# A hybrid encoder layer on one core: wide products of a unit ahead of its small ones, recurrence work moved from GpSimd to VectorE, and a new tail

## The chip, the cores and the metric

One core of a Trainium2 chip runs the whole layer. The metric is the device time of one execution in microseconds (us); lower is better. The engines are TensorE (PE, with its weight loads PEld), VectorE (DVE), ScalarE (ACT), GpSimd (POOL) and SyncE (SP), which issues most of the DMAs. Line numbers are those of the profiled kernel unless a text says that they are the changed kernel's.

## The reference

One layer for S = 256 tokens of width D = 2048, all in fp32:

```
x = x + 1/2 * SwiGLU_1(RMSNorm(x))                 # w1, w3: 2048 -> 5632, w2: 5632 -> 2048
h = RMSNorm(x);  [q | k | v | u | y] = h @ W_in     # 8 query heads, 2 kv heads of 128; u, y: 1024
A = attention(q, k, v), per-head RMS norm of q and k, axial rotary
u = centred depthwise conv of width 4 (u)
R = (RG-LRU_fwd(u) + RG-LRU_bwd(u)) * gelu(y)
x = x + concat([A, R]) @ W_out
x = x + 1/2 * SwiGLU_2(RMSNorm(x))
x = x + sigmoid(RMSNorm(x) @ W_gate) * (p @ W_ple)
out = RMSNorm(x)
```

The RG-LRU of one direction: r and i are sigmoids of u times block-diagonal matrices of 128 x 128 plus a bias; a = exp(c * r), where c comes from lambda; b = sqrt(1 - a^2) * i * u; and h[t] = a[t] * h[t-1] + b[t] along the tokens.

## The kernel before, in words

**Products.** The activations lie transposed, features on the partitions and the 256 tokens along a row. Every fp32 weight tile is split into a high part `whi` in fp32r (a cast on ACT, L83) and a low part `wlo` (a subtraction on VectorE, L84), and the activations likewise, as [hi | lo], 512 columns. A product is then a *wide* matmul, `whi` times 512 columns (L115), and a *small* one, `wlo` times the 256 hi columns (L117); `total` adds the two halves of the accumulator. `unit` makes 128 output features out of 16 weight tiles, or of two runs of 11 for w2. One 1 MB DMA on SP brings a unit's weights into one of three raw buffers, and two split pairs of eight tiles each go into a pool of four. Within a unit the order is 8 wide, 8 small, 8 wide, 8 small (for w2: 8, 8, 3, 3 in each run). After a unit `tick` moves every open job (a Python generator) one step on; the emitted instructions then get their final place on each engine from the Tile scheduler.

**Stages.** FFN1 runs to some 762 us: its lead takes the first units piece by piece with x, in pieces of 1, 1, 2, 4, 4, 4 blocks, the first three of them on ACT's DMA queue and the rest on SP's between the weight pieces. An FFN goes through the hidden width in two halves: 22 units of w1 and 22 of w3 give the hidden blocks `hT`, then 16 units of w2 add to x. Then the mixing stage, to 965 us, in this order: eight units of W_in for u, in two groups g of four, each followed by a convolution (L370) and the start of its `scan_job`; the projection of k and v; the two of q with rotary embedding; eight units for y; then wout, to 1055 us. FFN2 follows to some 1790 us, the gate with the embedding of p to 1890, and the tail.

**Scan job.** For a group of 512 features and both directions it makes four gate tiles: split uc and the gate weights (ACT and POOL), three fp32r products of 256 columns for each of 32 gate blocks over both jobs (L91 to L93), sigmoids (L403), products with c on POOL (L407), Exp and Tanh on ACT, i * u on POOL (L413), Sqrt on ACT, (a + 1) * r on VectorE (L419), times i * u on POOL (L421), four scans of 256 on VectorE (L424), and for both directions together the sum on POOL (L427). The final `y_job` multiplies with gelu(y) and splits into `mixT`, the activations of wout. POOL also scales u and y (L437, L574) and does one product of each rotary (L461).

**Tail.** The last two gate units keep their weights; their wide products come by halves of 128 tokens (L656), each followed by its features' sums, its norm (L209), a row of factors made on PE, and the scaling of all of x (L639) ahead of the stores. The output leaves in feature layout, which the host turns.

## Time and profile before

| | before |
|---|---|
| median of 3 runs | 1907.63 us (1907.08 to 1908.33) |
| the profiled execution | 1907.39 us, span 1905.6 us |
| PE / DVE / ACT / POOL busy | 98% / 63% / 51% / 15% of the span |
| mean granted clock of TensorE | 0.993 of full speed |
| HBM | 349 MB read, 2.1 MB written, 184 GB/s over the span |

The profile is of one execution, whose own time stands beside its span: a sum over its rows is made against that. Busy times of engines overlap. A matmul's end is modelled, so a run of matmuls is timed by the distance from its start to the start of the next run. A clock of 1.00 is TensorE at 2.4 GHz, the lower level is 1.2 GHz. In the waits, [0.71 <-DVE aT L88] means that the engine stood idle for 0.71 us, until VectorE's write of aT at line 88.

### The profile page before, as it was taken

Reading aid. Unit: us, or ns where it says so; the run is one execution under the profiler, and the core shown is the slowest. Engines: PE = TensorE matmul, PEld = TensorE weight load, DVE = VectorE, ACT = ScalarE, POOL = GpSimd, SP = SyncE. Lnnn points to the kernel's source line nnn. Section 1 sums busy time; section 2 is a strip of 40 time slices with the busy share of each in tenths; the row PEclk is TensorE's granted clock in tenths of the full one; section 3 lists DMA queues with packets and bytes.
Section 4 is the critical chain, followed back from the end, with each engine's and each line's share of the span. In section 5 each row is a group of like instructions: output and inputs, shape, how many; then the busy total and the mean of one; then the engine's idle time right before and its main releaser. Section 6 shows DMA issues by size and latency. Waiting matters only on the chain.

```text
span 1905.6 us, 27228 instructions
## 1 busy us (share of the span) xinstructions
PE 1872.7 (98%) x10632; PEld 1640.3 (86%) x10632; DVE 1203.6 (63%) x1723; ACT 965.2 (51%) x1494; POOL 292.6 (15%) x225
## 2 busy tenths in 40 slices
PE   9999999999999999988999999999999999999997
PEld 7888888888888888867878888888888888888886
DVE  6766655556566556888767666655555666655686
ACT  6544444444444445677654544444444444555553
POOL 0111100011111001564211111110001111101143
PEclk9999999999999999999999999999999999999998
DMA  8555545655555556544345555555565555555552
GB/s 316 205 189 187 192 160 190 210 199 179 197 180 176 182 184 213 175 152 155 133 152 181 191 185 194 182 186 167 194 208 196 181 195 184 202 197 195 201 177 67
DMA packets 61552, 352.85 MB, mean 185 GB/s; under 512 B 6512, under 2 KB 12144, under 8 KB 31088
## 3 DMA queue, kind: packets, MB, share of 16 engines
q1 hardware_dynamic: 60848, 350.51, 54.0%
q8 instruction: 83, 1.36, 0.3%
q10 hardware_dynamic: 576, 0.61, 0.1%
q14 instruction: 45, 0.37, 0.1%
HBM read 349.00 MB, written 2.10 MB: 184 GB/s over the span
## 4 chain that ended last, share of the span: by engine, by line
PE 92%; DVE 3%; ACT 3%; issue 1%; POOL 1%; DMA 0%; SPq 0%; POOLq 0%; DVEq 0%; ACTq 0%
PE acc L115 59%; PE acc L117 30%; DVE wlo L84 1%; DVE gate L424 1%; DVE uc L370 0%; ACT whi L83 0%; PE po L522 0%; PE acc L656 0%; PE pe L115 0%; POOL us L437 0%; DMA xs<-in_xT 0%; PE tr L495 0%; ACT gate L403 0%; ACT a L410 0%; ACT L416 0%
## 5 line engine op out<-in xcount | busy, mean ns | idle before, releaser
L84 DVE TENSOR_TENSOR wlo<-raw,whi 128x1024 fp32r<-128x1024 f32 x722 | 806.5, 1126 | 594.7 <-ACT whi L83 577.5
L83 ACT CAST whi<-raw 128x1024 fp32r<-128x1024 f32 x722 | 687.0, 952 | 814.5 <-PE acc L115 553.9
L115 PE MATMUL acc<-aT,whi 128*128 128x512 f32 x3296 | 832.0, 393 | 1.2 <-DVE aT L88 1.2
L115 PEld LDWEIGHTS acc<-aT,whi 128*128 128x128 f32 x3296 | 593.1, 189 | 107.8 <-DVE aT L88 2.7
L117 PEld LDWEIGHTS acc<-aT,wlo 128*128 128x128 f32 x3296 | 451.4, 191 | 32.7
L117 PE MATMUL acc<-aT,wlo 128*128 128x256 f32 x3296 | 463.0, 283 | 0.0
L115 PE MATMUL acc<-hT,whi 128*128 128x512 f32 x1408 | 364.8, 392 | 0.0
L304 POOL TENSOR_TENSOR s<-s,rB 128x256 f32<-128x256 f32 x88 | 123.8, 1407 | 1067.7 <-ACT s L301 1061.9
L115 PEld LDWEIGHTS acc<-hT,whi 128*128 128x128 f32 x1408 | 247.6, 189 | 37.2
L117 PEld LDWEIGHTS acc<-hT,wlo 128*128 128x128 f32 x1408 | 202.7, 190 | 21.3
L117 PE MATMUL acc<-hT,wlo 128*128 128x256 f32 x1408 | 209.0, 282 | 0.0
L246 POOL TENSOR_TENSOR ssq<-ssq,sqr 128x256 f32<-128x256 f32 x58 | 54.4, 939 | 339.6 <-ACT sqr L245 339.6
L115 PE MATMUL acc<-mixT,whi 128*128 128x512 f32 x256 | 64.6, 393 | 1.4 <-DVE mixT L84 1.4
L115 PEld LDWEIGHTS acc<-mixT,whi 128*128 128x128 f32 x256 | 45.9, 189 | 10.2 <-DVE mixT L84 2.1
L315 DVE SCALAR_TENSOR_TENSOR xs<-acc,xs 128x256 f32<-128x256 f32 x128 | 53.3, 417 | 0.0
L87 ACT ACTIVATE aT<-xs,par_sb 128x256 fp32r<-128x256 f32 x64 | 31.5, 506 | 41.9 <-DVE xs L315 39.3
L92 PE MATMUL acc<-wlo,aT 128*128 128x512 f32 x96 | 40.4, 421 | 11.3 <-DVE wlo L84 11.3
L88 DVE SCALAR_TENSOR_TENSOR aT<-xs,par_sb,aT 128x256 fp32r<-128x256 f32 x64 | 38.2, 610 | 19.4 <-ACT aT L87 19.1
L306 DVE TENSOR_TENSOR u<-u,s 128x256 f32<-128x256 f32 x88 | 37.4, 426 | 9.1 <-DVE u L149 0.5
L93 PE MATMUL acc<-whi,aT 128*128 128x512 f32 x96 | 39.8, 415 | 0.0
L84 DVE TENSOR_TENSOR hT<-u,hT 128x256 fp32r<-128x256 f32 x88 | 38.0, 431 | 1.9 <-ACT hT L83 1.9
L300 DVE TENSOR_TENSOR z<-z,rB 128x256 f32<-128x256 f32 x88 | 37.4, 425 | 2.7
(168 smaller groups left out, 1001.5 us busy)
## 6 DMA issues: line engine op xcount, KB each, us to landing
raw<-in_w2a SPq DMA_DIRECT2D x64, 704.0 KB, 4.0
raw<-in_w1b SPq DMA_DIRECT2D x44, 1024.0 KB, 4.8
raw<-in_w3b SPq DMA_DIRECT2D x44, 1024.0 KB, 4.9
raw<-in_w2b SPq DMA_DIRECT2D x64, 704.0 KB, 4.0
raw<-in_w3a SPq DMA_DIRECT2D x43, 1024.0 KB, 4.8
raw<-in_w1a SPq DMA_DIRECT2D x42, 1024.0 KB, 4.8
raw<-in_win SPq DMA_DIRECT2D x16, 1024.0 KB, 4.9
raw<-in_wout SPq DMA_DIRECT2D x16, 1024.0 KB, 4.8
```

The costliest lines, as they stand in the source:

```text
L83: nc.scalar.copy(hi, src)
L84: (eng or nc.vector).tensor_tensor(lo, src, f32(hi), op=ALU.subtract)
L88: nc.vector.scalar_tensor_tensor(lo, src, gain, f32(hi), op0=ALU.mult, op1=ALU.subtract)
L92: nc.tensor.matmul(ps, lhsT=ah, rhs=wl, start=False, stop=False)
L93: nc.tensor.matmul(ps, lhsT=al, rhs=wh, start=False, stop=last)
L115: nc.tensor.matmul(ps, lhsT=ws[i][0], rhs=acts[i], start=first and i == 0, stop=False)
L117: nc.tensor.matmul(ps[:, 1, :], lhsT=ws[i][1], rhs=acts[i][:, 0, :], start=False, stop=last and i == n - 1)
L246: (eng or nc.gpsimd).tensor_tensor(ssq[:, cols], ssq[:, cols], t, op=ALU.add)
L300: nc.vector.tensor_tensor(z, z, rB, op=ALU.mult)
L304: nc.gpsimd.tensor_tensor(s, s, rB, op=ALU.mult)
L306: nc.vector.tensor_tensor(u, u, s, op=ALU.mult)
L315: nc.vector.scalar_tensor_tensor(xs[:, n, :], ps[:, j, :], 0.5, xs[:, n, :], op0=ALU.mult, op1=ALU.add)
```

## The change

1. `unit` runs the wide products of all sixteen (or eleven) tiles of a weight load first, then all small ones; `tick` comes after each eight wide ones, so twice in a unit.
2. Lead: the parameters are loaded first, on SP; only the first two pieces of x go on ACT's queue (`EARLY` 3 to 2), the third goes on SP's; the ACT table load follows the first DMA; six warming products instead of eight.
3. `scan_job`: the gate products are plain fp32, without splits; the gate weights are loaded in halves in SP's order; every POOL operation is on VectorE; it yields at more points. The scalings by `rmB` and the rotary product go to VectorE too.
4. The order of mixing is u(0), k and v, u(1), q, y(0), y(1); `finish` runs open jobs to the point that y or wout needs. wout's rows are in another order on the host, and its first two units go by halves.
5. Tail: the features of both halves come back to back, squares and gains are on ACT, x is transposed on PE and scaled by the norm on the way out of PSUM, in eight pieces of 128x512 on ACT and VectorE; the output is in the layout of the reference.

```diff
-WARM = 8
...
+MIX_ORDER = [*range(4), *range(8, 12), *range(4, 8), *range(12, 16)]
...
+WARM = 6
...
-EARLY = 3
+EARLY = 2
...
+    def finish(done=lambda: not jobs):
+        while not done():
+            tick()
...
         at, n = 0, nk * len(srcs)
         for src in srcs:
             ws = weights(src, nk)
+            part = aT[at:at + nk]
             for j in range(0, nk, 8):
-                part = ws[j:j + 8]
-                unit_mms(ps, part, aT[at:at + len(part)], at == 0, at + len(part) == n)
-                at += len(part)
-        tick()
+                for i in range(j, min(nk, j + 8)):
+                    nc.tensor.matmul(ps, lhsT=ws[i][0], rhs=part[i], start=at + i == 0, stop=False)
+                tick()
+            for i in range(nk):
+                nc.tensor.matmul(ps[:, 1, :], lhsT=ws[i][1], rhs=part[i][:, 0, :], start=False,
+                                 stop=at + i == n - 1)
+            at += nk
         return ps
...
                         first=(g == 0 and k == 0), last=(g == n - 1 and k == 3))
-            tick()
+                if k % 2:
+                    tick()
         return ps
...
-    at = 0
-    for n in PIECES[:EARLY]:
-        load(flat(xs[:, at:at + n, :]), xT[:, at * S:(at + n) * S], nc.scalar)
-        if at == 0:
-            load(par_sb, par, nc.scalar)
-        at += n
+    load(par_sb, par)
+    load(flat(xs[:, 0:1, :]), xT[:, 0:S], nc.scalar)
     warm = sml.tile([P, 1], F32, tag="warm", name="warm", bufs=1)
     nc.gpsimd.memset(warm, 0.0)
     nc.scalar.activation(warm, warm, AF.Silu)
+    load(flat(xs[:, 1:2, :]), xT[:, S:2 * S], nc.scalar)
     zero = tok.tile([P, C], BF16, tag="tmp", name="zero", bufs=TMP)
     nc.vector.memset(zero, 0.0)
...
     def scan_job(g, u):
-        hi = mid.tile([P, 4, S], F32R, tag="mid", name="uc_hi")
-        lo = mid.tile([P, 4, S], F32R, tag="mid", name="uc_lo")
-        split(u, hi, lo, nc.gpsimd)
-        raw = wraw.tile([P, 4, C], F32, tag="raw", name="raw")
-        in_order(nc.sync.dma_start(flat(raw), lruw[g]), loads[-1])
-        yield
         gw = []
         for d in range(2):
-            wh = mid.tile([P, 2, C], F32R, tag="mid", name="gw_hi")
-            wl = mid.tile([P, 2, C], F32R, tag="mid", name="gw_lo")
-            split(raw[:, 2 * d:2 * d + 2, :], wh, wl, nc.gpsimd)
-            gw.append((wh, wl))
+            w = mid.tile([P, 2, C], F32, tag="mid", name="gw")
+            load(flat(w), lruw[g, :, 2 * C * d:2 * C * (d + 1)])
+            gw.append(w)
         yield
         r, i, a = [], [], []
         for d in range(2):
-            wh, wl = gw[d]
             for m in range(2):
...
-                        wc = slice(k * P, (k + 1) * P)
-                        mm3(ps[:, j, :], wh[:, m, wc], wl[:, m, wc], hi[:, k, :], lo[:, k, :],
-                            True, True)
+                        nc.tensor.matmul(ps[:, j, :], lhsT=gw[d][:, m, k * P:(k + 1) * P], rhs=u[:, k, :],
+                                         start=True, stop=True)
                     for j in range(2):
...
+                    yield
                 (r, i)[m].append(o)
-                yield
             cb = cneg[:, 8 * d + 4 * g:8 * d + 4 * g + 4].unsqueeze(2).broadcast_to([P, 4, S])
-            nc.gpsimd.tensor_tensor(r[d], r[d], cb, op=ALU.mult)
+            nc.vector.tensor_tensor(r[d], r[d], cb, op=ALU.mult)
+            yield
         for d in range(2):
...
-            nc.gpsimd.tensor_tensor(flat(i[d]), flat(i[d]), flat(u), op=ALU.mult)
-        yield
+            nc.vector.tensor_tensor(flat(i[d]), flat(i[d]), flat(u), op=ALU.mult)
+            yield
         for d in range(2):
...
-            nc.gpsimd.tensor_tensor(flat(r[d]), flat(r[d]), flat(i[d]), op=ALU.mult)
+            yield
+            nc.vector.tensor_tensor(flat(r[d]), flat(r[d]), flat(i[d]), op=ALU.mult)
+            yield
             for k in range(4):
...
-            yield
-        nc.gpsimd.tensor_tensor(flat(i[0]), flat(i[0]), flat(i[1]), op=ALU.add)
+                if k % 2:
+                    yield
+        nc.vector.tensor_tensor(flat(i[0]), flat(i[0]), flat(i[1]), op=ALU.add)
         hsum[g] = i[0]
     hsum = [None, None]
-    for g in range(2):
+    def u_part(g):
         u = mtile("uc")
...
-            nc.gpsimd.tensor_tensor(t, t, rmB, op=ALU.mult)
+            nc.vector.tensor_tensor(t, t, rmB, op=ALU.mult)
             conv(u[:, k, :], t, 4 * g + k)
         jobs.append(scan_job(g, u))
...
-        nc.gpsimd.tensor_tensor(sv, sv, cb, op=ALU.mult)
+        nc.vector.tensor_tensor(sv, sv, cb, op=ALU.mult)
...
+    u_part(0)
     v_sb = const.tile([P, NH, 2 * HD], F32, name="v_sb")
     pkv = proj(am, [wqkv[2, k] for k in range(4)])
...
-        dst = mix2[2 * qc + hp]
+        dst = mix2[2 * qc + hp] = mixtile()
...
-    mix2 = [mid.tile([P, 2, 2, S], F32R, tag="mid", name="mixT") for _ in range(NKD // 2)]
-    mixT = [mix2[k // 2][:, k % 2, :, :] for k in range(NKD)]
...
+    u_part(1)
     for qc in range(2):
...
-    def y_job(g, y):
-        for b in range(2):
-            part = y[:, 2 * b:2 * b + 2, :]
-            nc.scalar.activation(part, part, AF.Gelu_apprx_tanh)
-            nc.vector.tensor_tensor(part, part, hsum[g][:, 2 * b:2 * b + 2, :], op=ALU.mult)
-            dst = mix2[4 + 2 * g + b]
-            split(part, dst[:, :, 0, :], dst[:, :, 1, :])
+    def y_job(g, b, part):
+        nc.scalar.activation(part, part, AF.Gelu_apprx_tanh)
+        nc.vector.tensor_tensor(part, part, hsum[g][:, 2 * b:2 * b + 2, :], op=ALU.mult)
+        dst = mix2[4 + 2 * g + b] = mixtile()
+        split(part, dst[:, :, 0, :], dst[:, :, 1, :])
         yield
     for g in range(2):
+        finish(lambda: hsum[g] is not None)
         y = mtile("y")
...
-            nc.gpsimd.tensor_tensor(y[:, k, :], t, rmB, op=ALU.mult)
-        jobs.append(y_job(g, y))
-    tick()
+            nc.vector.tensor_tensor(y[:, k, :], t, rmB, op=ALU.mult)
+            if k % 2:
+                jobs.append(y_job(g, k // 2, y[:, k - 1:k + 1, :]))
     a2, ssq2 = act_tiles(), new_ssq()
+    first = [acc.tile([P, 2, S], F32, tag="acc", name="acc") for _ in range(2)]
+    raws = []
+    for n in range(2):
+        raws.append(wraw.tile([P, 16, P], F32, tag="raw", name="raw"))
+        load(flat(raws[n]), wout[n, 0])
+    for j in (0, 8):
+        if j:
+            finish()
+        for n in range(2):
+            hi, lo = spl_pair()
+            split(raws[n][:, j:j + 8, :], hi, lo)
+            blocks = [mix2[k // 2][:, k % 2, :, :] for k in MIX_ORDER[j:j + 8]]
+            unit_mms(first[n], [(hi[:, i, :], lo[:, i, :]) for i in range(8)], blocks, j == 0, j == 8)
+            tick()
+    order = [mix2[k // 2][:, k % 2, :, :] for k in MIX_ORDER]
     for n in range(NKD):
-        ps = unit(mixT, [wout[n, 0]], NKD)
+        ps = first[n] if n < 2 else unit(order, [wout[n, 0]], NKD)
         for j in (1, 0):
             nc.vector.tensor_tensor(xs[:, n, :], ps[:, j, :], xs[:, n, :], op=ALU.add)
...
         small.append(t)
-    for h in range(NH):
+    def last_features(h):
         cols = slice(h * P, (h + 1) * P)
+        pss = []
         for i in range(2):
...
+            pss.append(ps)
+        for i, ps in enumerate(pss):
             n = NKD - 2 + i
...
-            gated(n, g, pe[i], cols, nc.vector, last[i])
-        _, rf = inv_rms(ssq3, *last, halves=[h], keep=False)
-        if h == 0:
-            rows = tmp("rows")[:, :P]
-            nc.scalar.copy(rows, rf)
-            scale_out(0, rows, 0, nc.gpsimd)
+            x = xs[:, n, cols]
+            nc.scalar.activation(g, g, AF.Sigmoid)
+            nc.vector.tensor_tensor(g, g, pe[i][:, cols], op=ALU.mult)
+            nc.vector.tensor_tensor(x, x, g, op=ALU.add)
+            nc.scalar.activation(last[i][:, cols], x, AF.Square)
+            nc.scalar.activation(x, x, AF.Copy, scale=par_at(O_GF + n))
+    def norms(h):
+        cols = slice(h * P, (h + 1) * P)
+        ps = trp.tile([P, 2, S], F32, tag="tr", name="sums")
+        for j, q in enumerate((ssq3, *last)):
+            nc.tensor.matmul(ps[:, 0, 0:1], lhsT=q[:, cols], rhs=ones[:, 0:1], start=j == 0, stop=j == 2)
+        r = sml.tile([P, NH], F32, tag="inv", name="inv", bufs=2)[:, :1]
+        rsqrt(r, ps[:, 0, :1], D, 1)
+        return r
...
+    outs = {}
+    def put(h, b, ps, r):
+        if b % 2 == 0:
+            outs[h, b // 2] = mid.tile([P, 2, C], F32, tag="mid", name="out")
+        o = outs[h, b // 2][:, b % 2, :]
+        if b % 2:
+            nc.vector.tensor_scalar(o, ps, r, None, op0=ALU.mult)
+        else:
+            nc.scalar.activation(o, ps, AF.Copy, scale=r)
+        eng = nc.scalar if (h, b) == (1, 2) else nc.sync
+        eng.dma_start(out[h * P:(h + 1) * P, b * C:(b + 1) * C], o)
+    last_features(0)
+    last_features(1)
+    r0 = norms(0)
+    for b in range(4):
+        put(0, b, in_rows(0, b), r0)
+    ahead = [in_rows(1, b) for b in range(3)]
+    r1 = norms(1)
+    for b in range(3):
+        put(1, b, ahead[b], r1)
+    put(1, 3, in_rows(1, 3), r1)
```

`in_rows` transposes four blocks of x into a PSUM tile; the last features' products are as before.

TensorE at the end of FFN1's second half and the start of W_in. Before (`hT`: hidden blocks, `aT`: normed activations, `ssq`: sums of squares):

```order
L115 MATMUL acc<-hT,whi 128x512 x8
L117 MATMUL acc<-hT,wlo 128x256 x8
L115 MATMUL acc<-hT,whi 128x512 x3
L117 MATMUL acc<-hT,wlo 128x256 x3
L115 MATMUL acc<-aT,whi 128x512 x8
L117 MATMUL acc<-aT,wlo 128x256 x8
L115 MATMUL acc<-aT,whi 128x512 x15
L117 MATMUL acc<-aT,wlo 128x256 x8
L115 MATMUL acc<-aT,whi 128x512 x4
L219 MATMUL sums<-ones,ssq 128x1 x2
L115 MATMUL acc<-aT,whi 128x512
```

And now (L151 and L154 are the changed kernel's wide and small products):

```order
L151 MATMUL acc<-hT,whi 128x512 x11
L154 MATMUL acc<-hT,wlo 128x256 x11
L151 MATMUL acc<-aT,whi 128x512 x38
L154 MATMUL acc<-aT,wlo 128x256 x2
L228 MATMUL sums<-ones,ssq 128x1 x2
L154 MATMUL acc<-aT,wlo 128x256 x14
L151 MATMUL acc<-aT,whi 128x512
L154 MATMUL acc<-aT,wlo 128x256 x16
L151 MATMUL acc<-aT,whi 128x512 x8
L241 MATMUL rows<-dg,ones 128x128 x2
L151 MATMUL acc<-aT,whi 128x512
```

Runs of 8, 8, 3, 3 became 11 and 11, and those of 8 and 8 became 16 and 16 (the 38 wide ones are those of two units and six of a third; the small ones of the first two follow).

VectorE at the first scans of the mixing stage. Before (`wlo<-raw,whi`: splits, `gate<-a,gate`: L419's product and L424's scans):

```order
L84 TENSOR_TENSOR wlo<-raw,whi 128x1024 x4
L419 SCALAR_TENSOR_TENSOR gate<-a,gate 128x1024 x2
L84 TENSOR_TENSOR wlo<-raw,whi 128x1024
L424 SCALAR_TENSOR_TENSOR gate<-a,gate 128x256 x4
L84 TENSOR_TENSOR wlo<-raw,whi 128x1024
L424 SCALAR_TENSOR_TENSOR gate<-a,gate 128x256 x4
L84 TENSOR_TENSOR wlo<-raw,whi 128x1024
L209 TENSOR_SCALAR rs_v<-qss 128x2
L84 TENSOR_TENSOR wlo<-raw,whi 128x1024
L209 TENSOR_SCALAR rs_v<-qss 128x2
```

And now (L88 is the split, L418 the former L419, L421 the product that POOL made, L425 the scans, L440 the scaling that POOL made, L377 the convolution, L161 the sum of two halves):

```order
L418 SCALAR_TENSOR_TENSOR gate<-a,gate 128x1024
L88 TENSOR_TENSOR wlo<-raw,whi 128x1024
L421 TENSOR_TENSOR gate<-gate 128x1024
L418 SCALAR_TENSOR_TENSOR gate<-a,gate 128x1024
L377 SCALAR_TENSOR_TENSOR uc<-us,par_sb,uc 128x254
L161 TENSOR_TENSOR us<-acc,us 128x256
L88 TENSOR_TENSOR wlo<-raw,whi 128x1024
L425 SCALAR_TENSOR_TENSOR gate<-a,gate 128x256 x4
L421 TENSOR_TENSOR gate<-gate 128x1024
L377 SCALAR_TENSOR_TENSOR uc<-us,par_sb,uc 128x255
L88 TENSOR_TENSOR wlo<-raw,whi 128x1024
L440 TENSOR_TENSOR us<-us,rB 128x256
```

The scans now follow operations of VectorE's own, and the first scan job lies beside the convolutions of the second group.

VectorE in the tail. Before (L620 and L621: square and gain, L639: scaling of x, L209: the norm, L231: the diagonal of factors):

```order
L620 TENSOR_TENSOR last<-xs 128x128
L639 TENSOR_TENSOR xs<-xs,rows 128x4x128 x3
L621 TENSOR_SCALAR xs<-xs,par_sb 128x128
L209 TENSOR_SCALAR rs_v<-sums 128x1
L231 TENSOR_SCALAR dg<-ident,inv 128x128
L639 TENSOR_TENSOR xs<-xs,rows 128x2x128 x2
L639 TENSOR_TENSOR xs<-xs,rows 128x4x128 x3
```

And now (L674 to L679: the last features, L219: the norm, L709: scaling out of PSUM):

```order
L674 TENSOR_TENSOR small<-acc,small 128x128
L675 TENSOR_TENSOR small<-small,rB 128x128
L219 TENSOR_SCALAR rs_v<-sums 128x1
L678 TENSOR_TENSOR small<-small,pe 128x128
L679 TENSOR_TENSOR xs<-xs,small 128x128
L709 TENSOR_SCALAR out<-out,inv 128x512 x2
L219 TENSOR_SCALAR rs_v<-sums 128x1
L709 TENSOR_SCALAR out<-out,inv 128x512 x2
```

The long scalings between the two norms are gone; each norm now follows the features, and the output's scaling is shared with ACT.

## Rows read from the trace of the kernel before

**Rows 1.** Page, engines: busy us (share of span) xinstructions

```profile
PE 1872.7 (98%) x10632; PEld 1640.3 (86%) x10632; DVE 1203.6 (63%) x1723; ACT 965.2 (51%) x1494; POOL 292.6 (15%) x225
```

**Rows 2.** Stretches: us; busy us (x) of PE, PEld, DVE, ACT, POOL; PEclk; DMA share; GB/s

```profile
0.00:30.00 30.00, 27.61 (x125) 21.26 (x126) 20.20 (x39) 20.69 (x41) 0.92 (x9) 1.00 0.87 308
762.00:965.00 203.00, 185.19 (x948) 156.12 (x947) 158.22 (x194) 139.51 (x243) 89.17 (x48) 0.96 0.43 150
945.00:965.00 20.00, 15.40 (x70) 12.00 (x70) 10.44 (x21) 13.82 (x25) 0.72 (x1) 0.91 0.27 99
```

**Rows 3.** Timeline, mixing: start, us, engine, line, out<-in, xcount [idle before <-releaser]

```profile
832.14 6.74 DVE L424 TENSOR_TENSOR_SCAN gate<-a,gate 128x256 f32<-128x256 f32 x4
...
840.06 0.80 PE L92 MATMUL acc<-wlo,aT 128*128 128x512 f32 x1 [3.17 <-DVE wlo L84]
```

**Rows 4.** VectorE scans and splits in mixing: xcount, ns min/median/max

```profile
L424 DVE TENSOR_TENSOR_SCAN gate<-a,gate x16: 657/659/2881, 832.1 to 886.0; 128x256 f32<-128x256 f32 x16
...
L84 DVE TENSOR_TENSOR wlo<-raw,whi x51: 1194/1218/3433, 766.1 to 953.6; 128x1024 fp32r<-128x1024 f32 x51
```

**Rows 5.** Timeline of PE, 200 us: one half unit of w1

```profile
199.69 2.00 PE L115 MATMUL acc<-aT,whi 128*128 128x512 f32 x8
201.53 1.11 PE L117 MATMUL acc<-aT,wlo 128*128 128x256 f32 x8
```

**Rows 6.** Timeline of PE, 258 to 263 us: runs of w2

```profile
261.23 1.11 PE L117 MATMUL acc<-hT,wlo 128*128 128x256 f32 x8
...
262.18 0.86 PE L115 MATMUL acc<-hT,whi 128*128 128x512 f32 x3
...
262.88 0.52 PE L117 MATMUL acc<-hT,wlo 128*128 128x256 f32 x3
```

**Rows 7.** Timeline of PE at 750 us; chain of waits at 1879 us

```profile
749.50 3.59 PE L115 MATMUL acc<-aT,whi 128*128 128x512 f32 x15
752.92 1.12 PE L117 MATMUL acc<-aT,wlo 128*128 128x256 f32 x8
...
1878.87 3.84 PE small L647 x32
```

**Rows 8.** Timeline at the first w2 unit: PE and the last hidden block

```profile
255.56 2.00 PE L115 MATMUL acc<-hT,whi 128*128 128x512 f32 x8
...
257.72 0.43 DVE L84 TENSOR_TENSOR hT<-u,hT 128x256 fp32r<-128x256 f32 x1 [0.47 <-ACT hT L83]
```

**Rows 9.** Timeline of PE in the attention, 911 to 914 us

```profile
911.62 1.89 PE L522 MATMUL po<-pT_sb,v_sb 128*128 128x256 f32 x8
913.35 1.89 PE L495 MATMUL tr<-kT,qT 128*128 128x256 f32 x8
```

**Rows 10.** Groups by line and shape: a 256-wide product on POOL and on VectorE

```profile
L437 POOL TENSOR_TENSOR us<-us,rB 128x256 f32<-128x256 f32 x8 | 11.3, 1424 | 14.7 <-DVE us L149 9.3 <-ACT rB L236 5.4
...
L300 DVE TENSOR_TENSOR z<-z,rB 128x256 f32<-128x256 f32 x88 | 37.4, 425 | 2.7
```

**Rows 11.** Stretch 762 to 965 us, L424's and the splits' instructions alone

```profile
762.00:965.00 203.00, 18.28 (x16) 0.96 0.43 150
...
762.00:965.00 203.00, 71.94 (x315) 49.51 (x316) 77.03 (x52) 0.96 0.43 150
```

**Rows 12.** Timeline of the start: SP's issue and PE's wait

```profile
6.08 0.43 SPq L103 DMA_DIRECT2D xs<-in_xT  x1
...
12.88 2.39 PE L115 MATMUL acc<-aT,whi 128*128 128x512 f32 x7 [0.71 <-DVE aT L88]
```

**Rows 13.** Timeline of the tail, VectorE

```profile
1890.87 0.29 DVE L660 TENSOR_TENSOR small<-acc,small 128x128 f32<-128x128 f32 x1 [0.39 <-PE acc L656]
...
1893.43 2.95 DVE L639 TENSOR_TENSOR xs<-xs,rows 128x512 f32<-128x512 f32 x3
...
1896.50 0.14 DVE L209 TENSOR_SCALAR rs_v<-sums 128x1 f32<-128x1 f32 x1
...
1898.56 2.54 DVE L639 TENSOR_TENSOR xs<-xs,rows 128x256 f32<-128x256 f32 x5 [0.95 <-PE rows L232]
```

79 lines of the change are left out of this document (35 added, 44 removed).

## The prediction

> **What bounds the kernel now.** I read the engines' shares first. TensorE is busy for 98% of the span, so only three things can move the time: the number and spacing of its products, the few microseconds in which it stands still, and its two ends [rows 1]. The table by stretches then shows where it stands still. Between 762 and 965 us (the mixing stage) it works 185.19 of 203.00 us at a mean granted clock of 0.96: 17.8 us idle, and 0.04 x 203 = 8.1 us lost to stretches at the lower of its two clocks (1.2 instead of 2.4 GHz), 25.9 us in all [rows 2]. The end of that stage alone, 945 to 965 us, holds 20.00 - 15.40 = 4.6 us idle and 0.09 x 20 = 1.8 us of clock, 6.4 us; 19.5 us lie before it. The timeline inside the stage says what is late: at 840.06 a product waited 3.17 us for a low half from VectorE, which had just spent 6.74 us on four scans [rows 3]. Those scans have a median of 659 ns and a maximum of 2881 ns, the splits 1218 and 3433 ns [rows 4]; a scan has one size, so size is not the reason. The long ones lie where POOL (GpSimd) works on 1024-wide tiles.
>
> All terms are summed against the profiled execution, 1907.39 us (span 1905.6 us); the median of the runs, 1907.63 us, is 0.24 us above it, which I neglect. A measurement of this kernel can tell about 0.2%, 3.8 us, from no change.
>
> **Wide products first.** In a unit, eight wide products take 201.53 - 199.69 = 1.84 us [rows 5], eight small ones 262.18 - 261.23 = 0.95 us and three wide ones 0.70 us [rows 6]. Where the kernel already happens to run fifteen wide ones in a row they take 752.92 - 749.50 = 3.42 us, 0.228 each against 0.230 in runs of eight, and 32 small ones in a row take 3.84 us, 0.120 each against 0.119 [rows 7]. So the change of kind costs a few ns. Sixteen wide ones become 3.42 + 0.228 = 3.65 instead of 3.68 us (-0.03), sixteen small ones 1.92 instead of 1.90 (+0.01 to +0.02): I take -0.02 us for a unit of sixteen tiles, and -0.01 for a run of eleven. With 217 units (FFN, gate and mixing) and 128 runs (64 w2 units of two runs): -4.3 - 1.2 = **-5.5 us**, ends 0 and -8. The Trainium skill ("TensorE: Matmul & The Clock Gate", Back-to-back issue gap) lets the isolated spacing depend on the columns alone, so that the order is worth nothing, and this sum would be -14.9 us. The rows differ, if by only 2 ns a product; I go by them, and keep the other as a rival.
>
> **The wait that this adds.** The first w2 unit after w1 and w3 uses hidden block 10 while that block is still being made: the unit starts at 255.56, and the block's low half is done at 257.72 + 0.43 = 258.15, 2.59 us later [rows 8]. Before, its product comes after 8 wide, 8 small and 2 wide ones, at 1.84 + 0.95 + 0.46 = 3.25 us, so nothing waits. Now it comes after ten wide ones, at 2.29 us: 0.30 us of waiting, at four places (two halves of each FFN): **+1.2 us**, ends 0 and 2. Elsewhere a unit holds its four half pairs longer by some 2 us; VectorE and ScalarE need 1.2 us for a pair where PE needs 2.8, so I cost that at nothing.
>
> **Gates in fp32.** 96 products of 256 columns at 0.119 to 0.120 us (11.5 us) go, and 32 plain fp32 ones come. The value products of the attention have that form: eight records, two for each of four products, from 911.62 to 913.35, 0.433 each [rows 9]; 32 take 13.8 us: **+2.3 us** of PE, ends 2.0 and 2.6. Gone with them are the splits of the gate weights and of uc (six casts on ACT, six subtractions on POOL), which lie off the bound path here. The two lruw loads of each scan job now stand in SP's order ahead of weights; a raw buffer less is used, so I cost them at nothing; the cover is the third raw buffer.
>
> **VectorE takes POOL's work in the mixing stage.** Fourteen 1024-wide operations (L407, L413, L421, L427), at the 1.22 us of a free split [rows 4], sixteen 256-wide ones (L437, L574) at 0.425 instead of POOL's 1.424 [rows 10], and the rope products (four of 512, two of 256) at 0.85, an estimate as twice the 256-wide price, and 0.425: 17.1 + 6.8 + 4.3 = 28 us more on VectorE. Against that stands what POOL's neighbourhood costs it: the sixteen scans take 18.28 us where 16 x 0.659 = 10.5 would do, the 52 splits 77.03 where 52 x 1.218 = 63.3 would do [rows 11]: 7.7 + 13.7 = 21.4 us of stretch, if POOL is its cause. Net +7 us on 158.2 us of VectorE work in 203 us [rows 2]: it stays under PE's 185. The stalls, though, came from single late halves, and those chains get shorter: four scans 2.6 instead of 6.74 us [rows 3], a 256-wide POOL step of 1.4 us between two VectorE steps becomes 0.4 in the same queue [rows 10], and the finer steps of the scan job put splits between its operations (the order of VectorE above). New in that queue: a scan chain stands ahead of a split at every step, by at most two operations, 2.4 us, and PE has one unit's pairs (5.6 us) ahead of it; so a stall there needs two steps together.
> Putting kv between the u units and finishing g0 before y spreads the two scan jobs. What stays is the end of the attention, 6.4 us, since its last products still come right before wout; wout's first two units in halves give it a little work to do, but the second half holds the last attention blocks. For the middle I keep 4 of 19.5 us. Hence 25.9 - 10.4 = **-15.5 us**, ends -6 (a third of the middle) and -20 (nearly all of it).
> The Trainium skill ("Perfetto Trace Analysis", Optimizing Scalar/DVE Operations) advises the other direction, away from a saturated VectorE, even to GpSimd, but warns that the two share a port and that it might then not help. VectorE is at 158 of 203 us here, not saturated, and the stretched scans agree with the warning [rows 2, 4].
>
> **Start.** Two more transfers (the parameters and one piece of x) are issued by SP ahead of the four-block piece of x at 6.08 us. SP takes 0.43 us an issue, and the wait for that piece is what already holds PE 0.71 us at 12.88 [rows 12]; so each issue is paid in full: **+0.9 us**, ends -0.5 (par first and a table load off the queue help) and +3 (at 308 GB/s, [rows 2], the transfers can be late by more than the issue).
>
> **Tail.** From the last features at 1890.87, VectorE does three scalings (2.95 us) before the second half's norm at 1896.50, then five more, begun at 1898.56 and taking 2.54 us, and the span ends at 1905.6: 14.7 us [rows 13]. Now both halves' features come first, the norms follow directly, and eight pieces of 128x512 leave PSUM on two engines; the output's 2.1 MB need 6.8 us at 308 GB/s [rows 2]. I choose 3.2 us from the last features to the first piece sent, and 1 us behind the last one: about 11 us. **-3.8 us**, ends -1.5 and -5.5.
>
> **Sum.** -5.5 + 1.2 + 2.3 - 15.5 + 0.9 - 3.8 = -20.4: 1907.4 - 20.4 = **1887.0 us**.
>
> **Rivals.**
> A. The middle stalls don't shrink, because PE there waits for a chain whose length the other steps set (ACT's table loads, sigmoids). For it: VectorE gets 28 us more. Against: the row at 840.06 names a VectorE half. All but the mixing term: -4.9, 1902.5 us. 14 in 100.
> B. The middle stalls vanish altogether, as the scan jobs are spread; only the 6.4 us at the end stays: -24.4, 1883.0 us. For it: VectorE's free prices leave 20 us of slack. 17 in 100.
> C. Slower. The long scans and splits are not POOL's doing but come with VectorE's own queue or ACT's reads; then the 28 us come on top of 186 us and land where PE already waits, between u and y. VectorE would be the bound there: mixing grows instead of shrinking. Price: -4.9 + 28 = +23, 1930.5 us at full; it is slower than before as soon as the stalls grow by 5 us. Against it: unstretched scans (659 ns, the minimum 657) are the rule where POOL rests. 5 in 100.
> D. The order of products is worth nothing, as if a product's spacing hung on its columns alone: -14.9, 1892.5 us. For it: 2 ns on 230 is near what a timeline resolves, and the modelled ends hide it. 12 in 100.
>
> **How the numbers follow.** The forecast has the remaining 52 in 100. From 1877 (B with the low ends of order and tail) to 1900 (a third of the middle gained, and a worse start) lie nearly all of the forecast, B and D, and a small part of A: 8 in 10. Left out are most of A, C, and the extremes. Faster by over 0.2% (under 1903.8 us): all but C and the upper third of A, 0.90; within 0.2%: 0.05; slower: 0.05.
>
> **What would show it.** In the profile of the changed kernel: unit spacing of 5.57 instead of 5.59 us; a wait of about 0.3 us for hT in each first w2 unit; scans all near 0.66 us and splits near 1.22, with POOL almost empty in mixing; PE idle there near 8 us instead of 17.8, most of it before wout; the first pieces' wait near 1.6 us; about 11 us from last features to the end. The forecast is wrong if scans stay stretched with POOL idle, if PE waits for VectorE in the scans' steps for more than 10 us, or if the spacing of a unit does not move.

## The result, and the profile after

The changed kernel takes 1883.7 us (median of 4, 1882.59 to 1885.37) against 1907.98 us (median of 4): 0.9874 of the time, 95% interval 0.9857 to 0.9891, 24.3 us less. The forecast was 1887.0 us, in a range of 1877 to 1900, and faster. The profiled execution (1883.48 us) has a span of 1881.6 us. Its first lines, engines and TensorE's clock by fortieths of the span:

```profile
PE 1864.1 (99%) x10626; PEld 1640.7 (87%) x10626; DVE 1177.2 (63%) x1745; ACT 965.7 (51%) x1497; POOL 165.6 (9%) x181
...
PEclk9999999999999999999999999999999999999999
```

The stages, by the start of the first product of each, in us from the start of the span:

| from | before | after | the stage became shorter by |
|---|---|---|---|
| start to the first w2 product | 0 to 255.56 | 0 to 257.01 | -1.45 (longer) |
| w2, first half of FFN1 | 255.56 to 378.24 | 257.01 to 379.68 | 0.01 |
| w1 and w3, second half (44 units) | to 624.04 | to 624.61 | 0.87 |
| w2 | to 746.72 | to 747.27 | 0.02 |
| mixing and wout | to 1050.83 | to 1032.78 | 18.60 |
| FFN2's first 44 units | to 1297.52 | to 1278.62 | 0.85 |
| the rest of FFN2 | to 1788.67 | to 1768.91 | 0.86 |
| gate, to the last feature product | to 1890.55 | to 1870.13 | 0.66 |
| tail, to the end | to 1905.60 | to 1881.61 | 3.57 |

Three quarters of the gain lie in mixing. The table of stretches after, columns as in [rows 2]:

```profile
0.00:10.00 10.00, 6.24 (x24) 3.73 (x25) 4.34 (x14) 5.69 (x15) 0.92 (x9) 1.00 0.61 174
10.00:20.00 10.00, 7.21 (x33) 5.86 (x32) 5.97 (x12) 6.13 (x13) 0.00 (x0) 0.83 0.99 343
747.00:935.00 188.00, 187.71 (x979) 161.66 (x978) 142.98 (x223) 130.53 (x226) 8.49 (x8) 1.00 0.50 174
935.00:947.00 12.00, 7.88 (x30) 5.55 (x29) 6.68 (x18) 7.08 (x16) 0.00 (x0) 0.86 0.22 87
```

From 747 to 935 us PE works 187.71 of 188.00 us at full clock: of the 19.5 us that the middle had lost [rows 2], 0.3 us are left. What remains is the end of the attention, 12.00 - 7.88 = 4.1 us idle and 0.14 x 12 = 1.7 us of clock. The scans and the splits, as in [rows 4] (minimum, median, maximum in ns):

```profile
L425 DVE TENSOR_TENSOR_SCAN gate<-a,gate x16: 660/664/685, 831.7 to 909.0; 128x256 f32<-128x256 f32 x16
```

```profile
L88 DVE TENSOR_TENSOR wlo<-raw,whi x58: 1194/1219/1226, 764.1 to 961.1; 128x1024 fp32r<-128x1024 f32 x58
```

No scan and no split is stretched any more (685 and 1226 ns at most, against 2881 and 3433). VectorE got some 28 us of work more in mixing, and is yet busy for 162.75 us between 747 and 965 us, where it had 167.48 and the kernel got less far. First the kernel before, then the changed one (columns as in [rows 2]):

```profile
747.00:965.00 218.00, 200.19 (x1037) 169.43 (x1036) 167.48 (x208) 147.00 (x254) 91.15 (x50) 0.96 0.45 154
```

```profile
747.00:965.00 218.00, 213.59 (x1112) 183.15 (x1111) 162.75 (x259) 149.75 (x259) 9.83 (x10) 0.99 0.48 166
```

A unit and the first w2 unit, in PE's timeline, which answer to [rows 5] to [rows 8] (start, us, engine, line, out<-in, count):

```profile
195.78 3.82 PE L151 MATMUL acc<-aT,whi 128*128 128x512 f32 x16
199.43 2.08 PE L154 MATMUL acc<-aT,wlo 128*128 128x256 f32 x16
201.34 3.82 PE L151 MATMUL acc<-aT,whi 128*128 128x512 f32 x16
```

```profile
257.01 2.68 PE L151 MATMUL acc<-hT,whi 128*128 128x512 f32 x11
259.53 1.48 PE L154 MATMUL acc<-hT,wlo 128*128 128x256 f32 x11
260.84 1.32 PE L151 MATMUL acc<-hT,whi 128*128 128x512 f32 x5
```

A unit of sixteen tiles is 201.34 - 195.78 = 5.56 us, where two halves took 5.58 [rows 5, 6]. A run of eleven is 260.84 - 257.01 = 3.83 us, which the pieces of [rows 6] also give. There is no wait inside it. The start, which answers to [rows 12]:

```profile
6.39 0.43 SPq L111 DMA_DIRECT2D xs<-in_xT  x1
...
12.93 1.71 ACT L91 ACTIVATE aT<-xs,par_sb 128x256 fp32r<-128x256 f32 x4 [0.66 <-DMA xs<-in_xT]
...
14.02 3.33 PE L123 MATMUL acc<-aT,whi 128*128 128x512 f32 x7 [2.79 <-DVE aT L92]
```

And the tail, which answers to [rows 13]:

```profile
1870.86 0.28 DVE L674 TENSOR_TENSOR small<-acc,small 128x128 f32<-128x128 f32 x1
...
1872.79 1.27 ACT L711 ACTIVATE out<-out,inv 128x512 f32<-128x512 f32 x2 [0.86 <-POOL inv L220]
...
1873.50 4.28 SPq L713 DMA_DIRECT2D out<-out  x7
...
1875.76 1.41 DVE L709 TENSOR_SCALAR out<-out,inv 128x512 f32<-128x512 f32 x2 [0.68 <-POOL inv L220]
```

From the last feature at 1870.86 the first piece goes out at 1873.50, the last scaling ends at 1877.2, and the span at 1881.6: 10.75 us in place of 14.7.

### The profile page after: what moved, and what is told of

It reads as the page before. It is cut to its first block, busy times and chain, and to the rows that moved or that the text cites. A ratio compares the mean times of both kernels' runs of the same rounds, so it can differ in the third digit from the quotient of the medians.

```text
span 1881.6 us, 27187 instructions
## 1 busy us (share of the span) xinstructions
PE 1864.1 (99%) x10626; PEld 1640.7 (87%) x10626; DVE 1177.2 (63%) x1745; ACT 965.7 (51%) x1497; POOL 165.6 (9%) x181
## 4 chain that ended last, share of the span: by engine, by line
PE 97%; DVE 1%; ACT 1%; DMA 0%; issue 0%; SPq 0%; DVEq 0%; POOLq 0%; POOL 0%; ACTq 0%
PE acc L151 59%; PE acc L154 31%; PE acc L95 1%; PE acc L97 1%; PE acc L96 1%; PE acc L123 1%; PE tr L396 1%; DMA xs<-in_xT 0%; PE acc L125 0%; PE acc L668 0%; PE pe L123 0%; PE po L526 0%; PE tr L499 0%; PE small L657 0%; PE pe L125 0%
## 5 line engine op out<-in xcount | busy, mean ns | idle before, releaser
L88 DVE TENSOR_TENSOR wlo<-raw,whi 128x1024 fp32r<-128x1024 f32 x722 | 793.2, 1126 | 468.9 <-PE acc L154 283.7
L151 PE MATMUL acc<-aT,whi 128*128 128x512 f32 x3248 | 777.2, 391 | 0.0
L151 PEld LDWEIGHTS acc<-aT,whi 128*128 128x128 f32 x3248 | 596.9, 188 | 115.3
L154 PEld LDWEIGHTS acc<-aT,wlo 128*128 128x128 f32 x3248 | 416.8, 191 | 15.6
L154 PE MATMUL acc<-aT,wlo 128*128 128x256 f32 x3248 | 423.6, 283 | 0.0
L151 PE MATMUL acc<-hT,whi 128*128 128x512 f32 x1408 | 343.5, 391 | 0.0
L151 PEld LDWEIGHTS acc<-hT,whi 128*128 128x128 f32 x1408 | 256.3, 189 | 47.9
L154 PEld LDWEIGHTS acc<-hT,wlo 128*128 128x128 f32 x1408 | 185.8, 191 | 9.9
L154 PE MATMUL acc<-hT,wlo 128*128 128x256 f32 x1408 | 188.9, 282 | 0.0
L311 POOL TENSOR_TENSOR s<-s,rB 128x256 f32<-128x256 f32 x88 | 67.5, 767 | 1119.9 <-ACT s L308 1119.9
L253 POOL TENSOR_TENSOR ssq<-ssq,sqr 128x256 f32<-128x256 f32 x58 | 75.3, 1299 | 364.4 <-ACT sqr L252 358.3
L88 DVE TENSOR_TENSOR hT<-u,hT 128x256 fp32r<-128x256 f32 x88 | 38.0, 431 | 76.1 <-ACT hT L87 75.9
L92 DVE SCALAR_TENSOR_TENSOR aT<-xs,par_sb,aT 128x256 fp32r<-128x256 f32 x64 | 30.1, 483 | 63.3 <-ACT aT L91 63.3
L160 ACT COPY z<-acc 128x256 f32<-128x256 f32 x88 | 32.8, 373 | 69.5 <-PE acc L154 69.4
L160 ACT COPY u<-acc 128x256 f32<-128x256 f32 x88 | 32.7, 372 | 67.0 <-PE acc L154 67.0
L151 PE MATMUL acc<-mixT,whi 128*128 128x512 f32 x224 | 53.4, 391 | 0.0
L151 PEld LDWEIGHTS acc<-mixT,whi 128*128 128x128 f32 x224 | 41.2, 188 | 8.0
```

The costliest lines, as they stand in the source:

```text
L88: (eng or nc.vector).tensor_tensor(lo, src, f32(hi), op=ALU.subtract)
L92: nc.vector.scalar_tensor_tensor(lo, src, gain, f32(hi), op0=ALU.mult, op1=ALU.subtract)
L151: nc.tensor.matmul(ps, lhsT=ws[i][0], rhs=part[i], start=at + i == 0, stop=False)
L154: nc.tensor.matmul(ps[:, 1, :], lhsT=ws[i][1], rhs=part[i][:, 0, :], start=False, stop=at + i == n - 1)
L160: nc.scalar.copy(t, ps[:, 1, cols])
L253: nc.gpsimd.tensor_tensor(ssq, ssq, t, op=ALU.add)
```

## The experiments

Theories: **contention** (POOL's work in mixing stretches VectorE's beside it, and PE waits for the late halves), against **spreading** (the new order and the finer steps of the scan jobs remove the waits, on whichever engine the work is). For the order of products: place in the run, against columns alone. For the start: the queue, against shared throughput.

The runs are numbered in the order in which they were made; those that belong together stand together.

**Run 1: the order of products alone.** In the kernel before, `unit` becomes:

```diff
-            for j in range(0, nk, 8):
-                part = ws[j:j + 8]
-                unit_mms(ps, part, aT[at:at + len(part)], at == 0, at + len(part) == n)
-                at += len(part)
+            part = aT[at:at + nk]
+            for i in range(nk):
+                nc.tensor.matmul(ps, lhsT=ws[i][0], rhs=part[i], start=at + i == 0, stop=False)
+            for i in range(nk):
+                nc.tensor.matmul(ps[:, 1, :], lhsT=ws[i][1], rhs=part[i][:, 0, :], start=False,
+                                 stop=at + i == n - 1)
+            at += nk
```

> The kernel before, with the wide products of a unit first and nothing else. If the order saves 0.02 us a unit of sixteen tiles and nothing in w2 (first half of FFN1 was 0.9 us shorter over 44 units, w2's stretches unchanged): 219 units, -4.4 us, about 1903 us, and each stretch of 44 w1 and w3 units 0.87 us shorter than before. If a product's spacing hangs on its columns alone: those stretches equal to within 0.1 us, and no change in all. In mixing the stalls should stay near 26 us by both.

Measured: 1903.79 us, 0.9979 of before (0.9969 to 0.9988), -4.3 us; each stretch of 44 units 0.85 to 0.87 us shorter, w2's unchanged to 0.02 us. The place in the run counts: 0.02 us a unit, shown by itself. The starts in the trace (100 to 250 us) show where it lies: the first five spacings of a run of wide products are 228 to 236 ns and all later ones 227, 27 ns more for a run's beginning; of the small ones the first is 113 and the later ones 120, 7 ns less. A unit with one run of each kind instead of two saves the difference, 20 ns.

**Run 2: POOL's mixing work on VectorE, alone.** In the kernel before, at seven places (L407, L413, L421, L427, L437, L461, L574):

```diff
-            nc.gpsimd.tensor_tensor(r[d], r[d], cb, op=ALU.mult)
+            nc.vector.tensor_tensor(r[d], r[d], cb, op=ALU.mult)
```

> The kernel before, with the scan jobs' four POOL operations, the scalings of u and y and the rotary product on VectorE, and nothing else (POOL keeps the splits of the gate weights and uc). If POOL's wide operations stretch VectorE's and late halves follow from that: scans near 0.66 us, VectorE's busy time in mixing about 5 to 10 us more, the stalls of 26 us smaller by 8 to 18 us, some 1890 to 1900 us. If the spreading of the scan jobs is what counts, and not the engine: mixing within 4 us of before or longer, since VectorE has 28 us more in the same places; 1904 to 1925 us.

Measured: 1891.66 us, 0.9915 (0.9900 to 0.9930), -16.4 us; the stage from W_in to the end of wout 15.1 us shorter, with nothing spread. Scans and splits:

```profile
L424 DVE TENSOR_TENSOR_SCAN gate<-a,gate x16: 657/664/683, 828.8 to 879.4; 128x256 f32<-128x256 f32 x16
```

```profile
L84 DVE TENSOR_TENSOR wlo<-raw,whi x57: 1190/1218/3427, 765.7 to 964.4; 128x1024 fp32r<-128x1024 f32 x57
```

The scans are free; one split still takes 3.4 us, beside what POOL kept (the splits of uc and of the gate weights). VectorE's busy time between 747 and 965 us went from 167.48 to 173.51 us, although 28 us were added. Contention as predicted. What is left of the waits for low halves (1.33 us at 832.39, 0.73 at 844.3) lies in the projections, where each tile's low half is wanted right behind its high half (L91, L92); in the kernel before, all 11.3 us of waiting for low halves on PE (L92) lay there too, and none in a unit.

**Run 3: the work back on POOL in the changed kernel**, the reverse edit at the same seven places.

> The changed kernel, with the same seven kinds of operation back on POOL. If contention made the stalls: scans and splits stretched again (scans up to 2.9 us, splits up to 3.4), mixing 8 us or more longer than in the changed kernel, 1892 us and above. If the spreading of the jobs counts: mixing within 3 us of the changed kernel, 1881 to 1887 us, stretched operations or not.

Measured: 1892.43 us, 0.9923 (0.9907 to 0.9940), 8.7 us over the changed kernel; from W_in to the end of wout it is 293.17 us, against 285.51 in the changed kernel and 304.11 before.

```profile
L425 DVE TENSOR_TENSOR_SCAN gate<-a,gate x16: 657/660/2823, 836.4 to 911.4; 128x256 f32<-128x256 f32 x16
```

```profile
L88 DVE TENSOR_TENSOR wlo<-raw,whi x55: 1195/1224/3419, 764.2 to 964.9; 128x1024 fp32r<-128x1024 f32 x55
```

The stretch is back, and 7.7 us with it. But 10.9 us of the 18.6 stay: the gains overlap (15.1 us by the engine alone in run 2, 10.9 by the rest alone, 18.6 together). The rest is not spreading alone: the splits that the fp32 gates need no more are off POOL in this run too, which is busy for 69.01 us between 747 and 965 us, against 91.15 before. What spreading is worth by itself is read from run 6. The waits that are left name VectorE's halves again, 1.75 us at 836 us beside POOL's product of 2.57 us.

**Run 5: useless work on POOL** beside the changed kernel's scan jobs, seven 128-wide operations behind each of the fourteen wide products:

```diff
+    def extra(seen):
+        nc.gpsimd.tensor_tensor(spare, seen[:, 0, :P], seen[:, 0, :P], op=ALU.mult)
+        for _ in range(6):
+            nc.gpsimd.tensor_tensor(spare, spare, spare, op=ALU.subtract)
...
             nc.vector.tensor_tensor(r[d], r[d], cb, op=ALU.mult)
+            extra(r[d])
```

> The changed kernel, with useless work on POOL: behind each of the fourteen 1024-wide products of the scan jobs, seven 128-wide operations on a spare tile, the first of which reads a piece of the product; no result of POOL is used. If POOL's work stretches VectorE's by contention: scans and splits beside it take up to several times their free time again although nothing waits for POOL, and the mixing stage is 2 to 9 us longer than in the changed kernel, 1886 to 1893 us. If what POOL cost before was only the time of its own steps in the chain: VectorE's durations stay free, mixing within 1.5 us, about 1884 us.

Measured: 1888.01 us, 0.9893 (0.9876 to 0.9909), 4.3 us over the changed kernel.

```profile
L435 DVE TENSOR_TENSOR_SCAN gate<-a,gate x16: 674/818/884, 834.0 to 907.1; 128x256 f32<-128x256 f32 x16
```

```profile
747.00:965.00 218.00, 210.53 (x1092) 179.82 (x1092) 169.89 (x256) 145.29 (x254) 86.28 (x107) 0.99 0.47 164
```

The median scan went from 664 to 818 ns and VectorE from 162.75 to 169.89 us, with POOL busy for 86.28 us, nearly all on results nobody uses. So work on POOL slows VectorE by itself. That the scans reach 884 ns only, not 2.9 us, is a miss of the first expectation's size: here many short operations disturbed less than a few wide ones. The trace shows the two engines taking turns: a scan from 835.60 to 836.42, POOL's operation from 835.95 to 836.61, the next scan from 836.34 to 837.16. So a scan loses only the rest of one short operation (0.82 against 0.66 us), and POOL's 86.28 us hold waiting of its own. A small part of the 4.3 us can be the wait of a gate tile's next writer for POOL's one read of it.

**Run 6: VectorE and fp32 gates without the spreading**, that is run 2 and:

```diff
-                        mm3(ps[:, j, :], wh[:, m, wc], wl[:, m, wc], hi[:, k, :], lo[:, k, :],
-                            True, True)
+                        nc.tensor.matmul(ps[:, j, :], lhsT=gw[d][:, m, k * P:(k + 1) * P], rhs=u[:, k, :],
+                                         start=True, stop=True)
```

> The kernel before with POOL's mixing work on VectorE (as in the second run) and the gate products in plain fp32 without splits. If PE's extra time counts alone: 2.3 us more than that run, about 1894 us, the mixing stage 213 instead of 210.8 us. If the splits on POOL and ACT still stood behind the rest of its stalls (2.4 us between 830 and 845 us): these go, and the sum is within 1 us of it, 1891 to 1892.5 us.

Measured: 1896.43 us (1894.08 to 1897.53), 0.9938 (0.9924 to 0.9953), 4.8 us over run 2 (1.3 us in the mixing stages of the two profiles, one the slowest execution of run 2, the other the fastest of this). With POOL's splits gone no split is over 1227 ns:

```profile
L84 DVE TENSOR_TENSOR wlo<-raw,whi x56: 1201/1224/1227, 765.7 to 962.7; 128x1024 fp32r<-128x1024 f32 x56
```

```profile
859.94 2.43 DVE L415 TENSOR_TENSOR_SCAN gate<-a,gate 128x256 f32<-128x256 f32 x4
...
862.29 2.34 DVE L84 TENSOR_TENSOR wlo<-raw,whi 128x1024 fp32r<-128x1024 f32 x2
...
863.54 0.79 PE L92 MATMUL acc<-wlo,aT 128*128 128x512 f32 x1 [2.93 <-DVE wlo L84]
```

PE waits 2.93 us for a half that stands behind four scans of 2.43 us on VectorE, unstretched. Neither expectation met it: the products' 2.3 us and a new place for a wait. The changed kernel has no such wait, although four scans stand in a row there too (2.43 us at 907.28, with two splits right behind them). Its second job's scans, at 903.0 to 909.7 us, lie beside units of y; in run 6 they lie inside the projection of q, at 859.9 to 867.6. The first job's, at 831.7 to 840.6, lie inside that projection in the changed kernel too, without a wait. No run separates the new order of the jobs from the finer steps. The changed kernel is 12.7 us under this run, with the order of products (4.3) and the tail (3.4, below) among that, which leaves some 5 us for the two of them and the halves of wout, the two starts not counted; from W_in to the end of wout the profiles differ by 290.27 - 285.51 = 4.8 us.

**Runs 4, 10 and 11: the old start**, twice, the second time beside a repeat of the changed kernel:

```diff
-    load(par_sb, par)
-    load(flat(xs[:, 0:1, :]), xT[:, 0:S], nc.scalar)
+    for n in PIECES[:EARLY]:
+        load(flat(xs[:, at:at + n, :]), xT[:, at * S:(at + n) * S], nc.scalar)
...
+WARM = 8
+EARLY = 3
```

> The changed kernel, with the loads of the first pieces, the table load and the warming products as before (three pieces of x and the parameters on ACT's queue). If the start lost time because the third piece of x now stands in SP's queue: the first w2 unit starts at 254.7 us instead of 257.0, about 1881.4 us in all, 2.3 us under the changed kernel and 26.5 under the kernel before. If the loss comes from elsewhere (order of the products, other queues): it stays at 1883.7 us within 0.8 us.

> The changed kernel once more, for its start beside the next run: median 1883 to 1884.5 us; the four-block piece of x used from 12.4 to 13.3 us, and a clock of about 0.83 between 10 and 20 us.

> The changed kernel with the start of before once more (as in the fourth run), on the chip of the run ahead. If the old start is the better one, as the medians of the fourth run say: 1 to 2.5 us under the run ahead, and a four-block piece used at 11.4 to 12.3 us. If the start of the fourth run's profile is the usual one: equal to the run ahead within 0.8 us.

Measured: 1882.15 us (0.9869, 0.9854 to 0.9884) in run 4, 1882.67 (0.9866, 0.9851 to 0.9880) in run 11, where the repeat of the changed kernel gave 1884.83 (0.9877, 0.9862 to 0.9892). Medians: 1.6 and 2.2 us better; the intervals overlap. The first w2 product came at 257.28 and 255.14 us with the old start, and at 257.01 and 256.83 with the new; the four-block piece of x was used at 12.75 and 12.14, and at 12.93 and 12.25 us. One loading order gives landings half a microsecond apart. What divides the profiles is TensorE's clock between 10 and 20 us, behind the wait for that piece. It is 1.00 in run 11, and in run 9, which has the new start (255.41 us); it is 0.83, 1.7 us of the ten, in the changed kernel, its repeat and runs 3, 4, 5, 8 and 12, where w2 starts at 256.81 to 257.65. Either start shows both levels, so the medians' 2 us are not shown to come from the queue. (Run 4's profile is of its slowest execution, 1885.48 us.)

**Run 7: two more pieces of x on ACT's queue**, behind the table load:

```diff
+    for at, n in ((2, 2), (4, 4)):
+        load(flat(xs[:, at:at + n, :]), xT[:, at * S:(at + n) * S], nc.scalar)
+        in_order(loads[-1], hot)
-EARLY = 2
+EARLY = 4
```

> The changed kernel, with the third and fourth piece of x (two and four blocks) issued on ACT's queue right behind the table load, and off SP's. If the start waits for these pieces because they stand late in SP's queue: the waits of 1.8 and 2.8 us for them go, the clock does not fall between 10 and 20 us, and the first w2 unit starts at 253.5 to 255 us instead of 257.0; about 1881 us in all. If the transfers of x and of the weights share one throughput that is the limit: the waits move to the weight pieces, and the time stays within 1 us of 1883.7.

Measured: 1883.68 us (0.9874, 0.9859 to 0.9889), no change; first w2 product at 256.90 us. The wait for the fourth piece went, and PE waited 1.82, 0.39 and 0.68 us for high halves of weights (`whi`) between 5.7 and 10.7 us instead; the clock fell earlier, to 0.87 in the first ten us and 0.78 in the next. Moving a transfer to another queue moved the wait, as the second expectation has it. That shared throughput is the reason fits DMA engines busy for 0.97 of the time from 10 to 20 us, but in the first ten us it is 0.66, so it is not shown.

**Run 8: three units of wout by halves** (`range(2)` to `range(3)` at three places).

> The changed kernel, with three units of wout by halves instead of two, so 2.8 us more work for PE that does not need the last attention blocks. If the end of the attention (6 us of waits between 935 and 946 us) is only short of such work: these waits shrink by 2 to 2.8 us, about 1881 us. If the added splits stand ahead of the attention's steps on VectorE and ACT, so that the chain ends later by as much: within 1 us of 1883.7.

Measured: 1883.62 us (0.9872, 0.9858 to 0.9887), no change; from wout's first product to its last it is 102.0 us, against 101.9. The last value products start at 943.55 us instead of 942.14, and the waits are as long as before (2.00 us for the last one): the attention came later by what was put before it, the second expectation.

**Run 9: the old tail** in the changed kernel (`gated`, `scale_out` and the loop over halves as before, output in feature layout).

> The changed kernel, with the tail of the kernel before (features, norm and scaling half by half, output in feature layout). If the tail's gain is its own: 3.6 us more than the changed kernel, about 1887.3 us, and 15.0 instead of 11.5 us from the last feature products to the end. If part of it came from what lies ahead (the gate stage's order): less than 2 us more.

Measured: 1887.11 us (0.9887, 0.9871 to 0.9904), 3.4 us over the changed kernel, 2.3 over its repeat (run 10); 1870.58 to 1885.44, 14.9 us, from the last product of the features, against 11.5 in both profiles of the changed kernel. The tail's gain is its own.

**Run 12: idle products at the end of the attention**, over the old start:

```diff
+            for _ in range(3):
+                in_order(keep(), s_last[0])
+            for _ in range(4):
+                in_order(keep(), po_last[0])
```

`keep` is an fp32 product of the identity and v into a PSUM tile that nobody reads; `s_last` and `po_last` are the last products of scores and values.

> The changed kernel with the start of before (as in the fourth and eleventh run), and seven fp32 products of 256 columns whose result nobody uses in the waits at the end of the attention: three behind the last scores, four behind the last values. If the lower clock behind these waits is what differs between executions there (the stretch from 945 to 950 us had 0.66 in some profiles and 1.00 in others): the clock stays at 1.00 there, the first two units of wout end 1.5 to 2 us earlier than in the eleventh run (954.6 us with its start at 255.1), and the median falls to some 1880.5 to 1881.5 us. If the idle products only take PE's time ahead of the last attention steps: no gain, 1882 to 1883.5 us.

Measured: 1880.69 us (1880.45 to 1881.61), 0.9860 of before (0.9844 to 0.9877), 27.3 us under it: the lowest median of all, though its interval overlaps those of runs 4 and 11. The stretch from 945 to 950 us (columns as in [rows 2]), first of the repeat of the changed kernel, then of this one:

```profile
945.00:950.00 5.00, 3.78 (x15) 3.43 (x16) 3.74 (x6) 4.74 (x7) 0.00 (x0) 0.67 0.00 0
```

```profile
945.00:950.00 5.00, 5.00 (x32) 4.41 (x31) 4.01 (x6) 4.18 (x6) 0.00 (x0) 1.00 0.00 0
```

And the wait before the second halves, in the changed kernel and here:

```profile
946.33 0.74 PE L123 MATMUL acc<-mixT,whi 128*128 128x512 f32 x2 [2.00 <-DVE mixT L88]
```

```profile
942.36 1.89 PE L604 MATMUL kept<-v_sb,ident 128*128 128x256 f32 x8
944.52 0.73 PE L123 MATMUL acc<-mixT,whi 128*128 128x512 f32 x2 [0.27 <-DVE mixT L88]
```

The clock stayed at 1.00 where it was 0.67, that is, at 1.2 GHz for two thirds of the stretch. From wout's first product to its last it is 1032.52 - 929.02 = 103.5 us in run 11, 101.9 in the changed kernel's profile and 1030.95 - 930.66 = 100.3 here. In the changed kernel's own profile the lower clock came earlier, 0.92 and 0.74 from 935 to 940 and 940 to 945 us; here it is 1.00 all the way from 930 to 955. All four executions are shorter than the changed kernel's shortest (1882.59 us); some of that is the start. That the idle products keep the clock rests on one profile: run 5's, without them, also has 1.00 from 930 to 960 us, and 100.7 us from wout's first product to its last.

## Why the prediction was right, and where not

- **Sign, mechanism, range: right.** PE waited in mixing for halves from VectorE, VectorE was stretched by POOL, and moving POOL's work to VectorE took the stretch away (runs 2, 3, 5). VectorE did not become the bound; rivals A and C fell. The Trainium skill ("Perfetto Trace Analysis", Optimizing Scalar/DVE Operations) warns that work moved between these two engines may not help, as they share a port. The runs agree, and go further: with that work on POOL the stage was 15.1 us longer than in run 2; the port itself no run shows. Its advice to unload VectorE is for a saturated one, and here it was busy for 158 of 203 us [rows 2].
- **"For the middle I keep 4 of 19.5 us": too cautious.** 0.3 us were left. Rival B, 1883.0 us, is what came: from W_in to the end of wout -18.6 us; with 30 units of 0.02 us and the gates' 2.3 us taken out, the stalls lost 20.3 us, where I had -15.5. The step that failed is the choice of 4, made for splits behind two scan steps together. Run 6 shows such a wait, 2.93 us, where the jobs are not spread. In the changed kernel four scans and two splits in a row (907.28 to 911.95 us) delay no product: PE is in the units of y there, and no unit waited for a low half before either. That the new order is what counts, and not the finer steps, is not shown. The end of the attention was sized well, 5.8 us for 6.4.
- **Order of products: -4.3 us for 217 units, right** (0.87 for 44; run 1 alone gave -4.3). Rival D fell. The Trainium skill's formula for the isolated spacing, by the columns alone ("TensorE: Matmul & The Clock Gate", Back-to-back issue gap), would have left the stretches of 44 units as they were; they became 0.87 us shorter, and the measurement decides. The -1.2 us for the runs of eleven did not come: 3.83 us before and after. What the wide ones gain there, the small ones lose: 6 ns a run each.
- **"+1.2 us" for the last hidden block: wrong, by a wrong block.** The block that is late when w2 starts is the last of the 22 of this half, not block 10 [rows 8]. It belongs to the second run of eleven, whose wide products start 3.83 us after the first. So nothing waits, before or after. This error and the missing -1.2 us cancelled.
- **Gates: +2.3 us.** Two records of a plain fp32 product come 215 ns apart each in the trace, 0.43 us a product, as taken from [rows 9]. By run 6 the whole edit costs 4.8 us without spreading, where a wait comes up beside it.
- **Start: +0.9 us forecast.** In the two profiles it is 1.45 us, and with 41 shorter units (0.8 us) 2.3 us. PE waited 2.79 us for the piece, where the forecast's signs had 1.6, and 1.7 us of the loss is the clock that fell behind that wait (0.83 between 10 and 20 us, 1.00 before), for which the sum had no term. Profiles of kernels with one and the same start differ by up to 2.2 us, with that clock (255.41 us in run 9, 257.65 in run 5), so the size is not settled; the medians of runs 4 and 11 say 1.6 and 2.2. That each issue is paid in full was not shown: run 7 took the pieces off SP's queue, and the time stayed.
- **Tail: -3.8 us forecast, -3.6 measured** in the profiles, 3.4 by run 9 (2.3 beside the repeat).

## What to carry to other kernels

An engine that is far from saturated can still set the time by single late results; look at the maximum of a fixed-size operation, not at its mean, and at who worked beside it. Moving work from GpSimd to VectorE can lower VectorE's busy time, and with it the waits, where the two run side by side. Where PE must wait a few microseconds, products for nobody behind the last useful ones are worth a try: here they cost nothing, and the clock stayed up in the one profile taken.
